# Projecting the recurrent branch's gates by seven block products inside the stream of projections

## The chip, the cores and the metric

The kernel runs on one core of a Trainium2 chip. The time is the device time of one execution in microseconds (us); lower is better. Beside it there is a profile of one execution, which lists every instruction of every engine with its start, its duration and what it waited for. The engines are TensorE (PE in the profile, its weight loads PEld), VectorE (DVE), ScalarE (ACT), GpSimd (POOL) and SyncE (SP). Each of them takes its instructions strictly in the order in which they stand in its own queue, and an instruction that waits holds up all behind it on that engine.

## The reference

One layer of a decoder trunk with 1024 rows (tokens) and 1024 channels. The normalised and modulated input `h` is projected by one large matrix; two branches of linear attention run on the result, each is gated by a SiLU gate, projected, merged by sigmoid gates and projected once more.

```python
proj = h @ w_in[l]
hq, hf, hi, hz, gq, gk, gv, gz, ga, mg = jnp.split(proj, IN_OFFSETS, axis=-1)

def hgrn2_branch(hq, hf, hi, hz, lb, norm_w):       # the recurrent branch, 8 heads of 128 channels
    q = jax.nn.silu(hq)
    f = lb + (1.0 - lb) * jax.nn.sigmoid(fr)        # fr is hf in float32
    k = (1.0 - lb) * jax.nn.sigmoid(-fr)
    o = chunked_gated_linear_attention(q, k, v, log_f, 1.0)
    o = rms_norm(o.reshape(B, T, HGRN_WIDTH), norm_w)
    return o * jax.nn.silu(hz)
```

What the change touches is `hz`, the projection behind the recurrent branch's gate: 1024 rows times 1024 columns with 1024 terms each, an eighth of it for each of the 8 heads, and the product `o * silu(hz)`.

## The kernel before, in words

**Products.** Every float32 factor of a product is split into a high part that the fast matmul format holds exactly and the low rest, by a copy on ACT and a subtraction on DVE (`split`, L196 and L197; the same pair of instructions stands at L1263/L1264 in `build` and at L1285/L1286 in `prep_duo`). A product is three matmuls: high times high, high times low, low times high.

**The stream.** After the normalisation of the rows a list of jobs runs (`Stream.go`). A `Feat` projects 128 columns for all 1024 rows: 8 steps over the terms, each of three products by two halves of the rows, 48 matmuls of 128x512 (L541), and then a closing function (`silu_done` at L952 and L953 for queries and gates, `hf_done` at L1077 to L1081 for the forget gates). The second branch's heads come first; then, for each recurrent head h from 0 to 7, the `Feat` of the query (hq), that of the forget gate (hf), for h = 0 and 4 the values of four heads (`Vblk2`), and the `Feat` of the gate (hz). `ahead` loads weights two jobs ahead and splits them one job ahead.

**The side tracks.** At each step of a job `weave` lets two queues of generators go on by a unit: the attention of the heads that have their inputs (scores at L683 to L781 on PE with masks and decays on DVE between them, L690 to L785; transposes L807; the products with the values L829, L848, L850), and in the back `gate_side` (the output gate, L1054) and `prepare`. `prepare` forms, for a later stage, sums of quarters of `h` (`factors`) and of quarters of the weights (`weight_sums`, four DVE additions L1195 to L1199 and four stores by POOL's queue, L1201, for each of 16 pieces), and waits while fewer than 12 buffers are free. A head's attention ends with `post`: on ACT a square (L1095), and on DVE `(attention * norm weight) * gate` (L1096).

**The last stages.** Four matrix products of 1024 x 1024 x 1024 (the two merging gates and the two branch projections) are each made by seven products of quarters instead of eight (`PRODUCTS`, in the order 1, 2, 5, 3, 6, 7, 4). A `Pair` holds the accumulator banks of two 128-column blocks; `Pair.run` is 12 matmuls of 128x512 for one product (L1343), and `Pair.after` carries sums from one product to the next: `snap_of` copies a bank to SBUF (L1315, L1317), `seed` copies such a copy back into a bank (L1323), `summed` adds on DVE (L1330). The output projection (L1520) closes the kernel.

**The order.** After the first 110 us or so no order written by hand holds: the tile framework's scheduler decides, when the kernel is built, where each instruction stands in its engine's queue. On the chip these queues are then fixed. In the rows of order shown below a name such as `b339_5089` is one buffer in one use, `pd124_4758` a pair of PSUM banks.

Of the kernel before, what the change touches and what calls it, by code (L numbers as in the profile page):

```python
# [31 lines left out]
OUT_PRODUCTS = (1, 5, 3, 6, 7, 2, 4)  # L32

# [50 lines left out]
def hybrid_trunk_kernel(  # L84
# [772 lines left out]
    class Stream:  # L857
# [186 lines left out]
    def gate_side():  # L1044

        gacc, gbias = S.get([D]), S.get([D])
# [38 lines left out]

    def hgrn_attention(h):
        st = h_state
        y = [None]
        sq = [None]

        def post(vh, half, po):
# [4 lines left out]
            nc.vector.scalar_tensor_tensor(y[0][:, sl], po, vec[:, R_HN + h:R_HN + h + 1],  # L1096
                                           y[0][:, sl], ALU.mult, ALU.mult)
# [5 lines left out]
        put_act(yh_d, h, y[0])  # L1103
        if ssq[0] is None:
            ssq[0] = sq[0]
        else:
            nc.gpsimd.tensor_add(ssq[0], ssq[0], sq[0])
            S.free(sq[0])
        if h == 7:
            yield 2  # L1110
            rst = S.get([T])
            yield from inverse_root(rst, ssq[0], D)
            S.free(ssq[0])
            rst_h[0] = rst

# [7 lines left out]
    for h in range(8):  # L1123
# [9 lines left out]
        J.append(Feat(col(C_HZ + h * P), rhs_h, silu_done(h_state, ("z", h))))  # L1133
# [19 lines left out]
    f_x = new_factors(h_d, "fx")  # L1153

    def factors(acts, f):
        sub = nc.vector.tensor_sub
        for kk in range(2):
            while len(S.free_list) < 12:
                yield 1
# [19 lines left out]
    sources += [[branch(n, d) for d in range(0, 8, 2)] for n in (1, 0)]  # L1179

    w_sums = [[[dp.tile([P, T], F32, name=f"ws{b}{j}{i}") for i in range(4)] for j in range(2)] for b in range(4)]

    def weight_sums(b, i):
        src = sources[b][i]
        while len(S.free_list) < 12:
            yield 1
# [12 lines left out]
        add(parts[3], parts[6], x2[:, :, 0])  # L1199
# [3 lines left out]
        S.free(x1, x2, s1, s2)  # L1203
        yield 3

    def prepare():
        yield from factors(h_d, f_x)
        for b in range(4):
# [15 lines left out]
    outs = [None] * 4  # L1224
# [45 lines left out]
    def load_duo(b, p, j):  # L1270

        t = raw_w[b, p, j] = S.get([2, 512])
        if p in SUMS:
            nc.sync.dma_start(t.rearrange("p a f -> p (a f)"), w_sums[b][j][SUMS[p]])
# [7 lines left out]
    def prep_duo(*duo):  # L1282
        t = raw_w.pop(duo)
        hi, lo = S.get([2, 512], F32R), S.get([2, 512], F32R)
# [3 lines left out]
        wt[duo] = (hi, lo)  # L1288

# [17 lines left out]
    class Pair:  # L1307
# [24 lines left out]

        def run(self, p):
            if p in (1, 5):
# [3 lines left out]
            h = H[0 if self.b == 1 else self.b, p]  # L1338
            for kt in range(4):
                h_hi, h_lo = (z[kt // 2][:, kt % 2, :] for z in h)  # L1340
                sl = slice(kt * P, (kt + 1) * P)
                for n, (a, c) in enumerate(((hi, h_hi), (hi, h_lo), (lo, h_hi))):
                    nc.tensor.matmul(o, a[:, sl], c, start=(p in (1, 5) and kt == 0 and n == 0),  # L1343
                                     stop=(kt == 3 and n == 2), skip_group_check=True)
                if kt % 2:
                    stream.weave(1)
# [3 lines left out]
        def after(self, p):  # L1350
            bank, snap, out = self.bank, self.snap, outs[self.b]
            if p == 1:
                if self.b:
# [88 lines left out]
    outs[:] = [put_gate1, put_gate0, put_t1, put_m]  # L1442
# [276 lines left out]
```

## Time and profile before

| | |
|---|---|
| median of 3 runs | 1215.8 us (1215.12 to 1216.45) |
| profiled execution: its time, its span | 1216.46 us, 1214.8 us |
| PE busy, share of the span | 1184.1 us, 97% |
| DVE | 790.9 us, 65% |
| ACT | 546.9 us, 45% |
| POOL | 123.8 us, 10% |
| stretch of the stream with the recurrent heads | 366 to 806 us |
| last stages, output stage | 806 to 1130 us, 1130 to 1207 us |

"Busy" counts an engine's instructions while they run. Consecutive instructions overlap a little at their ends, so that what a row of them costs in line is read from the distance of their starts. The time of a run is some 1.7 us longer than the span of its profile.

### The profile page before, as it was taken

The numbers are of one execution on the slowest core, as the hardware profiler recorded it, in microseconds if no ns is written. First come the engines' busy times: TensorE is split into PE (matmuls) and PEld (weight loads), VectorE is DVE, ScalarE is ACT, GpSimd is POOL, SyncE is SP. The second block draws the span as 40 slices with busy tenths as digits, with TensorE's granted clock in tenths as the row PEclk, the third lists the DMA queues.
The fourth block names the chain that finished last, engine by engine and source line by source line (L and its number), as shares of the span: only waits on it lengthen the run. The fifth ranks groups of instructions, "written<-read, shape, count | busy, mean of one in ns | idle before, by whom it ended". The sixth has DMA issues, their size and how long they took to land.

```text
span 1214.8 us, 20860 instructions
## 1 busy us (share of the span) xinstructions
PE 1184.1 (97%) x8579; PEld 982.6 (81%) x8579; DVE 790.9 (65%) x1245; ACT 546.9 (45%) x797; POOL 123.8 (10%) x215
## 2 busy tenths in 40 slices
PE   5999999999999999999999999999999999999997
PEld 3777889889798888888887888877778888878886
DVE  4637444774848456877884365794653775988994
ACT  5646732434434244344332324455743544444554
POOL 4100000202111121121110101011220000000000
PEclk9999999999999999999999999999999999999999
DMA  9814000844444267255341112054697746435523
GB/s 320 277 70 139 18 19 19 293 141 161 156 152 149 66 207 249 94 179 169 108 174 47 59 53 70 36 174 158 227 343 277 260 160 208 135 104 173 174 104 122
DMA packets 130961, 183.51 MB, mean 151 GB/s; under 512 B 7467, under 2 KB 97633, under 8 KB 130866
## 3 DMA queue, kind: packets, MB, share of 16 engines
q1 hardware_dynamic: 117250, 136.87, 35.7%
q0 software_dynamic: 13568, 45.31, 9.6%
q8 instruction: 67, 1.10, 0.4%
q14 instruction: 28, 0.23, 0.1%
q10 hardware_dynamic: 48, 0.01, 0.0%
HBM read 132.87 MB, written 49.28 MB: 150 GB/s over the span
## 4 chain that ended last, share of the span: by engine, by line
PE 61%; issue 23%; DVE 3%; ACT 3%; POOL 2%; DMA 1%; POOLq 0%; ACTq 0%; DVEq 0%
PE pd L541 19%; PE pd L1343 9%; PE sc_ps L1343 5%; PE pm L1343 5%; PE pd L1520 3%; PE pd L643 2%; PE pd L644 2%; PE pd L645 2%; PE sc_ps L1520 2%; PE pm L848 1%; PE pd L352 1%; PE pm L829 1%; PE pm L850 1%; PE pm L1520 1%; PE sc_ps L352 1%
## 5 line engine op out<-in xcount | busy, mean ns | idle before, releaser
L541 PE MATMUL pd<-b,b 128*128 128x512 f32 x1632 | 387.4, 394 | 0.0
L541 PEld LDWEIGHTS pd<-b,b 128*128 128x128 f32 x1632 | 302.4, 188 | 64.8 <-issue 1.4
L1343 PE MATMUL pd<-b,b 128*128 128x512 f32 x720 | 173.7, 392 | 4.3 <-ACT b L1414 2.1
L1343 PEld LDWEIGHTS pd<-b,b 128*128 128x128 f32 x720 | 133.7, 188 | 35.7 <-ACT b L1414 3.2
L197 DVE TENSOR_TENSOR b<-b,b 128x1024 fp32r<-128x1024 f32 (+2 forms) x89 | 98.9, 1122 | 83.1 <-ACT b L196 65.4
L196 ACT CAST b<-b 128x1024 fp32r<-128x1024 f32 (+2 forms) x89 | 82.9, 948 | 92.1 <-DVE b L1199 14.6
L1286 DVE TENSOR_TENSOR b<-b,b 128x1024 fp32r<-128x1024 f32 x56 | 68.3, 1224 | 66.9 <-ACT b L1285 52.3
L1285 ACT CAST b<-b 128x1024 fp32r<-128x1024 f32 x56 | 58.3, 1050 | 73.9 <-PE pd L1343 20.6
L1343 PE MATMUL sc_ps<-b,b 128*128 128x512 f32 x324 | 79.4, 391 | 1.0 <-ACT scT L793 1.0
L600 PE MATMUL pd<-b,b 128*128 128x256 f32 x256 | 74.2, 290 | 0.0
L1264 DVE TENSOR_TENSOR b<-b,b 128x1024 fp32r<-128x1024 f32 x48 | 59.2, 1251 | 20.8 <-ACT b L1263 15.1
L602 PE MATMUL pd<-b,b 128*128 128x256 f32 x256 | 72.5, 283 | 0.0
L601 PE MATMUL pd<-b,b 128*128 128x256 f32 x256 | 72.4, 283 | 0.0
L1343 PEld LDWEIGHTS sc_ps<-b,b 128*128 128x128 f32 x324 | 60.3, 188 | 14.6 <-ACT scT L793 1.4
L1343 PE MATMUL pm<-b,b 128*128 128x512 f32 x300 | 72.1, 389 | 0.0
L1263 ACT CAST b<-b 128x1024 fp32r<-128x1024 f32 x48 | 49.9, 1050 | 41.2 <-PE pd L1343 16.0
L1343 PEld LDWEIGHTS pm<-b,b 128*128 128x128 f32 x300 | 56.3, 188 | 11.7
L352 PE MATMUL pd<-b,b 128*128 128x512 f32 x192 | 53.3, 410 | 2.0 <-ACT b L196 0.9
L1201 POOL DMA_DIRECT2D ws<-b x64 | 34.6, 541 | 192.0 <-DVE b L1195 86.5
L735 ACT COPY xb<-b 128x512 f32<-128x512 f32 x48 | 29.4, 620 | 49.4 <-PE sc_ps L715 26.7
L643 PE MATMUL pd<-b,b 128*128 128x512 f32 x128 | 51.3, 401 | 0.0
L644 PE MATMUL pd<-b,b 128*128 128x512 f32 x128 | 50.0, 390 | 0.0
(285 smaller groups left out, 1964.3 us busy)
## 6 DMA issues: line engine op xcount, KB each, us to landing
b<-in_w_in_dram SPq DMA_DIRECT2D x66, 512.0 KB, 4.2
ws<-b POOLq DMA_DIRECT2D x64, 256.0 KB, 3.3
b<-ws SPq DMA_DIRECT2D x32, 512.0 KB, 4.9
b<-in_x_dram SPq DMA_DIRECT2D x16, 512.0 KB, 5.7
b<-in_ada_w_dram SPq DMA_DIRECT2D x32, 256.0 KB, 6.9
b<-in_w_branch_dram SPq DMA_DIRECT2D x16, 512.0 KB, 4.4
b<-h SPq DMA_DIRECT2D x14, 512.0 KB, 4.3
wo<-b POOLq DMA_DIRECT2D x14, 512.0 KB, 5.7
```

What stands on the lines that cost most here:

```text
L196: nc.scalar.copy(hi, src)
L197: nc.vector.tensor_sub(lo, src, hi.bitcast(F32))
L352: nc.tensor.matmul(accs[f], wg(a, d, f), b[d][:, half * 512:half * 512 + 512], start=(d == 0 and n == 0), stop=(d == KT - 1 and n == 2))
L541: nc.tensor.matmul(ps[0:w, th * 512:(th + 1) * 512], a[:, k, 0:w], b[:, th * 512:(th + 1) * 512], start=(k == 0 and n == 0), stop=(k == KT ...
L600: nc.tensor.matmul(o, lh, hi[:, k % 4, :], start=(k == 0), stop=False)
L601: nc.tensor.matmul(o, lh, lo[:, k % 4, :], start=False, stop=False)
L602: nc.tensor.matmul(o, ll, hi[:, k % 4, :], start=False, stop=(k == KT - 1))
L643: nc.tensor.matmul(o, lh, hi[:, k % 2, :], start=(k == 0), stop=False)
L644: nc.tensor.matmul(o, lh, lo[:, k % 2, :], start=False, stop=False)
L1286: nc.vector.tensor_sub(lo, t, hi.bitcast(F32))
L1343: nc.tensor.matmul(o, a[:, sl], c, start=(p in (1, 5) and kt == 0 and n == 0), stop=(kt == 3 and n == 2), skip_group_check=True)
L1520: nc.tensor.matmul(o, a, b, start=(p in (1, 5) and kt == 0 and n == 0), stop=(kt == 3 and n == 2), skip_group_check=True)
```

## The change

The eight gate `Feat`s of the recurrent heads (8 x 48 = 384 matmuls) go. In their place two jobs `Gates` stand in the stream, one behind hf of head 2 and one behind hf of head 6. Each makes the gates of four heads by the seven block products of the last stages: two `Pair`s, 7 products, 12 matmuls each, so 2 x 7 x 12 = 168, and 336 in both (L1462 in the changed file).

For that a `Gates` takes both pairs of PSUM accumulators that the `Feat`s use in turn, loads and splits seven weight pieces (three of them plain quarters, four of them sums that four further calls of `weight_sums` have to form earlier), fetches four pairs of summed factors and splits them (L197/L198, 8 splits; the plain quarters use the split input that is there), and runs `Pair.after`'s copies, seeds and sums (L1427, L1425, L1433, L1440). Its results leave by `put_z`: a sigmoid on ACT and a product on DVE for each 512 rows (L1145, L1146). While a `Gates` runs, `prepare` and `gate_side` pause, since they ask for more free buffers than there are; outside of it they ask for 10.

Heads 0, 1, 2 and 4, 5, 6 end their attention before or while their gate is made. Where it isn't there yet, ACT scales the attention's result (L1110), it is kept, and when gate and result both are there one product on DVE joins them (`gate_y`, L1092). Behind hf of head 7 there is no gate `Feat` any more, so this head's attention runs wholly inside the last stages.

Lines of the changed file are up to 120 further down than those of before; up to the scoring lines it is one line (L197 becomes L198, L541 becomes L542), L1343 becomes L1462, L1330 becomes L1440, L1317 becomes L1427.

**PE at the place of the first `Gates`.** Before, behind hf of head 2, the gate `Feat` of that head (accumulator `pd132`) begins:

```order
L541 MATMUL pd132_4977<-b5_143,b294_4897 128x512 x2
L541 MATMUL pd132_4977<-b13_151,b294_4897 128x512 x2
L541 MATMUL pd132_4977<-b5_143,b295_4898 128x512 x2
L541 MATMUL pd132_4977<-b6_144,b294_4897 128x512 x2
L541 MATMUL pd132_4977<-b14_152,b294_4897 128x512 x2
L541 MATMUL pd132_4977<-b6_144,b295_4898 128x512 x2
```

A product here needs the weights (`b294`, high part, `b295`, low part), split a job earlier. In the changed order the same queue stands as follows where product 6 of the first `Gates` gives way to product 7 (the accumulators are halves of `pd124` and `pd125`; `b322` to `b325`, `b334` and `b335` are split factors; `b328`, `b329` are product 6's weights and `b338` (high), `b339` (low) those of product 7):

```order
L1462 MATMUL pd124_4758<-b325_5012,b328_5032 128x512
L1462 MATMUL pd124_4758<-b324_5011,b329_5033 128x512
L1462 MATMUL pd124_4758<-b324_5011,b328_5032 128x512
L1462 MATMUL pd124_4758<-b325_5012,b328_5032 128x512
L1462 MATMUL pd124_4758<-b324_5011,b329_5033 128x512
L716 MATMUL sc_ps_72<-xb_142,b293_4750 32x48 x5
L1462 MATMUL pd125_4759<-b334_5080,b338_5088 128x512
L1462 MATMUL pd125_4759<-b335_5081,b338_5088 128x512
L1462 MATMUL pd124_4758<-b334_5080,b338_5088 128x512
L1462 MATMUL pd125_4759<-b334_5080,b339_5089 128x512
```

The third matmul of product 7 on `pd125` is the first that needs `b339`; ten matmuls of product 6 (the second pair's, with two short pieces of scoring) stand between the end of the first pair's product 6 and product 7.

**DVE at the same place.** Before, this part of DVE's queue, beside the same `Feat`, holds scoring, the gate's own product (L953) and weight sums:

```order
L699 TENSOR_TENSOR b301_4969<-b301_4969,b300_4968 128x256x3
L695 COPY_PREDICATED blk_141<-mask1_683,sc_ps_72 128x64
L696 COPY_PREDICATED blk_141<-mask1_683,sc_ps_72 128x64x2
L711 TENSOR_TENSOR xb_142<-xb_142,tot0_725 128x64x4
L697 COPY_PREDICATED blk_141<-mask1_683,sc_ps_72 128x64x2
L717 TENSOR_TENSOR b291_4849<-xb_142,tot0_725 128x64x12
L698 COPY_PREDICATED blk_141<-mask1_683,sc_ps_72 128x64
L953 TENSOR_TENSOR b309_5099<-b309_5099,pd132_4977 128x1024
L718 TENSOR_TENSOR tot0_725<-tot0_725 128x64
L1195 TENSOR_TENSOR b324_5384<-b317_5310 128x512
L719 TENSOR_TENSOR tot0_725<-tot0_725 128x64
L1198 TENSOR_TENSOR b323_5383<-b324_5384,b318_5311 128x512
```

In the changed order `b339` is written by the last of these rows. The first `Gates`' sum behind product 6 of the first pair (L1440 on `b333`) stands 13 rows ahead of it, followed by L691 and these:

```order
L700 TENSOR_TENSOR b293_4750<-b293_4750,b292_4749 128x256x3
L1146 TENSOR_TENSOR b307_4892<-b307_4892,b333_5072 128x512
L696 COPY_PREDICATED blk_141<-mask1_683,sc_ps_72 128x64
L1092 TENSOR_TENSOR b307_4892<-b307_4892,b279_4500 128x1024
L697 COPY_PREDICATED blk_141<-mask1_683,sc_ps_72 128x64x2
L198 TENSOR_TENSOR b347_5181<-b332_5057,b346_5180 128x1024
L198 TENSOR_TENSOR b337_5085<-b327_5016,b336_5084 128x1024
L698 COPY_PREDICATED blk_141<-mask1_683,sc_ps_72 128x64x2
L198 TENSOR_TENSOR b349_5185<-b330_5053,b348_5184 128x1024
L699 COPY_PREDICATED blk_141<-mask1_683,sc_ps_72 128x64
L1440 TENSOR_TENSOR b340_5151<-b340_5151,pd124_4758 128x512
L198 TENSOR_TENSOR b339_5089<-b321_5005,b338_5088 128x1024
```

Between the two stand the splits of product 4's weights and factors (`b347`, `b349`), of a factor of product 7 (`b337`), a gate's closing products (L1146, L1092), the second pair's sum (L1440) and scoring.

On ACT the copy that writes `b338` stands seven rows behind the copy of product 6's bank (L1427, to `b333`), and five of the rows between are copies for other splits.

**The second `Gates`, DVE.** The low part of product 7's weights is the last row here (`b490`); L1440 on the first pair's product 6 stands 19 rows ahead of it:

```order
L1092 TENSOR_TENSOR b460_6969<-b460_6969,b423_6480 128x1024
L198 TENSOR_TENSOR b488_7180<-b478_7070,b487_7179 128x1024
L757 COPY_PREDICATED blk_141<-mask4_700,sc_ps_72 128x8x4
L758 COPY_PREDICATED blk_141<-mask4_700,sc_ps_72 128x8x8
L744 TENSOR_TENSOR b444_6868<-b444_6868,tot0_725 128x32x16
L759 COPY_PREDICATED blk_141<-mask4_700,sc_ps_72 128x8x8
L745 TENSOR_TENSOR b437_6674<-b437_6674,tot0_725 128x32x16
L760 COPY_PREDICATED blk_141<-mask4_700,sc_ps_72 128x8x4
L757 COPY_PREDICATED blk_141<-mask4_700,sc_ps_72 128x8x4
L758 COPY_PREDICATED blk_141<-mask4_700,sc_ps_72 128x8x8
L744 TENSOR_TENSOR b444_6868<-b444_6868,tot0_725 128x16x32
L198 TENSOR_TENSOR b490_7184<-b472_7059,b489_7183 128x1024
```

Scoring of head 6 (L757 to L759, L744, L745) stands between them beside the splits. Two products earlier in the same job, the low part of product 5's weights (`b462`) is the last of these rows, behind the closing products of hf of head 6 (L1082 to L1084) and that head's scoring:

```order
L198 TENSOR_TENSOR b459_6954<-b448_6882,b458_6953 128x1024
L1082 TENSOR_SCALAR b443_6867<-b443_6867,oml_676,lb_675 128x1024
L1083 TENSOR_SCALAR b443_6867<-b443_6867 128x1024
L744 TENSOR_TENSOR b431_6550<-b431_6550,tot1_726 128x8x64
L745 TENSOR_TENSOR b420_6459<-b420_6459,tot1_726 128x8x64
L786 COPY_PREDICATED blk_141<-mask16_717,sc_ps_72 128x8x16
L1084 TENSOR_SCALAR b444_6868<-b444_6868,oml_676 128x1024
L677 TENSOR_TENSOR xb_142<-b437_6674,b443_6867 128x32x8
L678 TENSOR_TENSOR xb_142<-b437_6674,b443_6867 128x32x8x2
L198 TENSOR_TENSOR b462_6973<-b449_6885,b461_6972 128x1024
```

and PE needs it at the last of these rows, after one product's 12 matmuls and a transposition:

```order
L1462 MATMUL pd163_6876<-b8_146,b441_6769 128x512
L1462 MATMUL pd163_6876<-b16_154,b441_6769 128x512
L1462 MATMUL pd163_6876<-b8_146,b442_6770 128x512
L808 MATMUL pm165_6912<-ident_73,b431_6550 128x128 x4
L808 MATMUL pm166_6918<-ident_73,b431_6550 128x128 x3
L1462 MATMUL pd164_6877<-b456_6949,b461_6972 128x512
L1462 MATMUL pd164_6877<-b457_6950,b461_6972 128x512
L1462 MATMUL pd164_6877<-b456_6949,b462_6973 128x512
```

The diff, cut to its core:

```diff
@@ Stream.go
-                    if u >= 3 and u % 2:
+                    if u >= getattr(job, "late", 3) and u % 2:
@@ gate_side
+        while len(S.free_list) < room[0]:
+            yield 1
@@ hgrn_attention
             if half == 0:
-                y[0], sq[0] = st.pop(("z", h)), S.get([T])
+                y[0], sq[0] = st.pop(("z", h), None), S.get([T])
+                if y[0] is None:
+                    y[0], plain[0] = S.get([T]), True
...
+            if plain[0]:
+                nc.scalar.activation(y[0][:, sl], po, AF.Copy, scale=vec[:, R_HN + h:R_HN + h + 1])
+            else:
+                nc.vector.scalar_tensor_tensor(y[0][:, sl], po, vec[:, R_HN + h:R_HN + h + 1],
+                                               y[0][:, sl], ALU.mult, ALU.mult)
...
+    class Gates:
+        raws, parts, late = 1, 2, 20
...
+        def run(self):
+            j = self.j
+            two = [Pair(ZB, 2 * j + i) for i in range(2)]
+            room[0] = N_SLOTS
+            ps = [dtile(), dtile()]
+            R.free_list.extend(t[:, i * 512:i * 512 + 512] for t in ps for i in range(2))
+            load_duo(ZB, PRODUCTS[1], j)
+            self.fetch(5)
+            for n, p in enumerate(PRODUCTS):
+                if n + 2 < len(PRODUCTS):
+                    load_duo(ZB, PRODUCTS[n + 2], j)
+                if p in (2, 3):
+                    self.build({2: 5, 3: 6}[p])
+                if p in (5, 3, 6):
+                    self.fetch({5: 6, 3: 7, 6: 4}[p])
+                for i, pair in enumerate(two):
+                    yield from pair.steps(p)
+                    pair.after(p)
+                    if p == 5:
+                        pair.seed()
+                    if i == 0:
+                        if p in (6, 7):
+                            self.build({6: 7, 7: 4}[p])
+                        if n + 1 < len(PRODUCTS):
+                            prep_duo(ZB, PRODUCTS[n + 1], j)
...
@@ the list of jobs
-        J.append(Feat(col(C_HZ + h * P), rhs_h, silu_done(h_state, ("z", h))))
+        if h in (2, 6):
+            J.append(Gates(h // 4))
...
@@ prepare
-        for b in range(4):
+        for b in (ZB, 0, 1, 2, 3):
             for i in range(4):
                 yield from weight_sums(b, i)
```

More of the change, by code (lines that the diff above doesn't have):

```diff
@@ L1102, in hgrn_attention @@
             S.free(*st.pop(("v", h // 4)))
-        put_act(yh_d, h, y[0])
+        if plain[0]:
+            st[("y", h)] = y[0]
+            gate_y(h)
+        else:
+            put_act(yh_d, h, y[0])
         if ssq[0] is None:
@@ L1153, in hybrid_trunk_kernel @@
     f_x = new_factors(h_d, "fx")
+    room = [10]
     def factors(acts, f):
@@ L1157, in factors @@
         for kk in range(2):
-            while len(S.free_list) < 12:
+            while len(S.free_list) < room[0]:
                 yield 1
@@ L1331, in summed, with part, steps @@
             outs[self.b](2 * self.i + f, half, t, True)
+        def part(self, p, kt):
+            if self.b == ZB and p in (1, 2, 3):
+                kh, half = ((0, 0), (1, 0), (1, 1))[p - 1]
+                return [z[kh * 4 + kt][:, half * 512:half * 512 + 512] for z in (h_hi, h_lo)]
+            return [z[kt // 2][:, kt % 2, :] for z in H[0 if self.b == 1 else self.b, p]]
         def run(self, p):
+            for _ in self.steps(p):
+                stream.weave(1)
+        def steps(self, p):
             if p in (1, 5):
```

77 lines of the change are left out of this document (65 added, 12 removed).

## The prediction

> **What bounds the kernel now.** I read the page first (busy shares, then the costliest groups), then the stretches of the program one by one, the waits of PE in the stream, and the timelines of PE and DVE at the place of the change.
>
> ```profile
> PE 1184.1 (97%) x8579; PEld 982.6 (81%) x8579; DVE 790.9 (65%) x1245; ACT 546.9 (45%) x797; POOL 123.8 (10%) x215
> L541 PE MATMUL pd<-b,b 128*128 128x512 f32 x1632 | 387.4, 394 | 0.0
> L1343 PE MATMUL pd<-b,b 128*128 128x512 f32 x720 | 173.7, 392 | 4.3 <-ACT b L1414 2.1
> ```
>
> PE is busy 97% of the span, and the stream's matmuls (L541) had no idle time before them. By stretches (columns: stretch, its length, busy PE, PEld, DVE, ACT, POOL, granted clock, DMA share, GB/s):
>
> ```profile
> 450.00:614.00 164.00, 163.41 (x1629) 135.90 (x1628) 123.97 (x236) 64.88 (x109) 26.32 (x42) 1.00 0.47 152
> 535.00:550.80 15.80, 15.80 (x129) 12.79 (x127) 15.68 (x27) 3.24 (x5) 3.19 (x6) 1.00 0.76 252
> 870.00:1130.00 260.00, 257.74 (x1132) 211.34 (x1131) 185.68 (x197) 121.86 (x153) 13.41 (x25) 1.00 0.63 208
> ```
>
> So matmuls that go are time that goes, as long as nothing makes PE wait in their place. DVE has room on average (124 of 164 us in the first heads), but none just where the first `Gates` comes: 535 to 550.8 is the gate `Feat` of head 2, and there DVE worked 15.7 of 15.8 us. PE didn't wait for it, because what a `Feat` needs was split a job earlier. The waits of PE between 366 and 806 us are these two:
>
> ```profile
> PE pm L829 <- ACT b L808: 0.4, 1, 0.4
> PE sc_ps L715 <- DVE blk L698: 0.2, 1, 0.2
> ```
>
> **What the change takes away.** 384 matmuls against 336. The price of one, from the timeline of PE at that `Feat` (start, duration, line, count):
>
> ```profile
> 531.60 11.18 PE L541 MATMUL pd<-b,b 128*128 128x512 f32 x48
> 542.71 1.31 PE L683 MATMUL sc_ps<-xb,b 128*32 128x80 f32 x64
> 543.95 7.09 PE L541 MATMUL pd<-b,b 128*128 128x512 f32 x30
> 551.24 0.89 PE L715 MATMUL sc_ps<-xb,b 128*32 128x48 f32 x64 [0.20 <-DVE blk L698]
> 552.06 8.45 PE L541 MATMUL pd<-b,b 128*128 128x512 f32 x36
> ```
>
> From start to start 48 take 11.11 us, 0.23 each. The 48 that go are worth 11.1 us, all of it on the path. Scoring costs 1.24/64 = 0.02 (L683) and 0.82/64 = 0.013 (L715) per matmul.
>
> **What it adds: product 7 has to wait.** The `Feat`s had a job's time for splitting. A `Gates` has one product's, two pairs by 12 matmuls, 24 x 0.23 = 5.5 us, for one weight split, two factor splits and the sums, with the attention's scoring in the same queue. The order shows where this ends last: at product 7. PE's third matmul of it needs `b339`, the low part of its weights, and DVE makes this 13 rows behind the sum (L1440) that itself waits for the first pair's product 6. The prices are from DVE's timeline at the start of the last stages, where the same lines run back to back, by start to start:
>
> ```profile
> 806.08 1.23 DVE L1286 TENSOR_TENSOR b<-b,b 128x1024 fp32r<-128x1024 f32 x1
> 807.21 1.23 DVE L1264 TENSOR_TENSOR b<-b,b 128x1024 fp32r<-128x1024 f32 x1
> ...
> 811.75 0.43 DVE L690 TENSOR_TENSOR blk<-sc_ps,eye 128x256 f32<-128x256 f32 x1
> 812.08 0.96 DVE L699 TENSOR_TENSOR b<-b,b 128x768 f32<-128x768 f32 x1
> 812.95 0.45 DVE L695 COPY_PREDICATED blk<-mask,sc_ps 128x64 f32<-128x64 int32 x1
> 813.13 0.56 DVE L696 COPY_PREDICATED blk<-mask,sc_ps 128x128 f32<-128x128 int32 x1
> 813.47 0.74 DVE L710 TENSOR_TENSOR xb<-b,tot 128x512 f32<-128x512 f32 x1
> 814.11 0.46 DVE L697 COPY_PREDICATED blk<-mask,sc_ps 128x128 f32<-128x128 int32 x1
> 814.34 0.47 DVE L711 TENSOR_TENSOR xb<-xb,tot 128x256 f32<-128x256 f32 x1
> 814.71 0.45 DVE L698 COPY_PREDICATED blk<-mask,sc_ps 128x64 f32<-128x64 int32 x1
> 814.88 1.34 DVE L1286 TENSOR_TENSOR b<-b,b 128x1024 fp32r<-128x1024 f32 x1
> ...
> 817.61 0.28 DVE L721 TENSOR_TENSOR tot<-tot 128x64 f32<-128x64 f32 x1
> 817.93 0.60 DVE L746 TENSOR_TENSOR tot<-tot 128x32 f32<-128x32 f32 x3
> 818.52 0.96 DVE L720 TENSOR_TENSOR b<-b,tot 128x768 f32<-128x768 f32 x1
> 819.39 0.19 DVE L756 COPY_PREDICATED blk<-mask,sc_ps 128x32 f32<-128x32 int32 x1
> 819.49 0.23 DVE L757 COPY_PREDICATED blk<-mask,sc_ps 128x64 f32<-128x64 int32 x1
> 819.62 0.69 DVE L744 TENSOR_TENSOR b<-b,tot 128x512 f32<-128x512 f32 x1
> 820.23 0.22 DVE L758 COPY_PREDICATED blk<-mask,sc_ps 128x64 f32<-128x64 int32 x1
> ```
>
> A 1024 wide row costs 1.13, a 512 wide one 0.60 (819.62 to 820.23), and the copy of a bank on ACT, as the last stages make it (L1317), this:
>
> ```profile
> L1317 ACT ACTIVATE b<-pd 128x512 f32<-128x512 f32 x12 | 7.0, 592 | 4.7 <-PE pd L1343 4.7
> L1263 ACT CAST b<-b 128x1024 fp32r<-128x1024 f32 x39 | 40.6, 1049 | 34.4 <-PE pd L1343 16.0 <-DMA b<-fx 5.1 <-PE pm L1343 5.0
> ```
>
> First `Gates`, counted from the end of the first pair's product 6: the copy 0.59; then on DVE L1440 0.60, L691 0.33, L700 0.87, L1146 0.60, L696 0.18, L1092 1.13, L697 0.34, two splits 2.26, L698 0.23, a split 1.13, L699 0.17, L1440 0.60, and the split of `b339` 1.23 to its end: 10.3 us. ACT isn't later: its copy of the high part comes behind four wide copies and two narrow ones, about 5 x 1.05 + 3 x 0.59 = 7.0. PE has meanwhile ten matmuls of product 6, three of product 7 (13 x 0.23 = 3.0) and twelve short ones (0.2). It waits 10.3 - 3.2 = **7.1 us**, in two pieces (for the high part, then for the low one).
>
> Second `Gates`, the same join, DVE's 19 rows behind L1440 there: copy 0.59, L1440 0.60, the three short kinds L722 and L747 0.9, five 1024 or 768 wide rows and the 512 wide L1146 among them (1.13 + 0.60 + 0.87 + 1.13 + 1.13 = 4.9), scoring L757 to L745 with three wide ones (0.1 to 0.13 each, 0.61 each wide) 2.5, the split of `b490` 1.23: 10.7 us. PE has 14 matmuls and 32 short ones, 3.2 + 0.4 = 3.6. It waits **7.1 us**. Both ends for either wait: zero (DVE takes these rows while PE is still at product 6, which the order excludes, since the sum at their head waits for product 6 itself) and 10.7. I take the sums, as they are rows of exactly these kinds.
>
> **At product 5 of the second `Gates`** PE needs `b462` after 14 matmuls and a transposition like this one:
>
> ```profile
> 831.68 0.92 PE L807 MATMUL pm<-ident,b 128*128 128x128 f32 x7
> ```
>
> That is 14 x 0.23 + 0.9 = 4.1 us behind the scoring matmuls (L782) with which the `Gates` begins. DVE's rows from the first that needs these, L744, to `b462` are two of 512 at 0.60, L786 0.2, L1084, L677 and L678 (bounded by 0.60 and 1.13 each, mostly the first) and the split 1.23: 4.4 to 6.0. L1082 and L1083 ahead of them, up to 1.13 each, may be done by then or not. So the wait is between 0.3 and 4.2 us; I take **2.0**.
>
> **What else it adds.** Per `Gates` 15 splits instead of 4, eight sums and eight gate products of 512, against four gate products of 1024 (L953) saved: on DVE 11 x 1.13 + 16 x 0.60 - 4 x 1.13 = 17.5 us more within PE's 45 us. What is put off meets the next head's transpositions and values behind the `Gates` (L808, L830, L849 of the changed file). PE waited 0.6 us in all for such things in this stretch before; the other bound is the 17.5. I take 1.5 each, **3.0**, near the low end, as DVE was idle 40 us of 164 there. The weight sums are the same DVE and POOL work moved from one place of the queue to another, with 4 more of them: 4 x 4 x 0.60 = 9.6 us of DVE and 16 stores on POOL's queue, under PE's matmuls of the heads; if that cover goes they appear in the 1.5. They are queued on POOL and the fetches on SP; the weight piece of product 7 is asked for two products early (11 us), against 4.9 us that such a load takes:
>
> ```profile
> b<-ws SPq DMA_DIRECT2D x32, 512.0 KB, 4.9
> ```
>
> **Behind the stream.** Head 7's attention has eight steps of a `Feat` less to hide under and runs with the first groups of the last stages, whose DVE is 71% busy (185.7 of 260). Before, PE lost 64.0 - 61.0 = 3.0 us between 806 and 870:
>
> ```profile
> 806.00:870.00 64.00, 60.99 (x508) 48.64 (x508) 40.40 (x62) 39.64 (x60) 6.29 (x8) 1.00 0.50 177
> 811.90 5.73 PE L1343 MATMUL pd<-b,b 128*128 128x512 f32 x24 [1.49 <-DVE b L953]
> ```
>
> The 1.49 for L953, head 7's gate, goes; more scoring joins comes. I take **+0.5**, with ends -1.5 and +3. ACT's plain scaling in place of a DVE product, and `gate_side`'s eight DVE rows at a later place, lie off PE's path; I cost them at nothing.
>
> **Sum.** -11.1 + 7.1 + 7.1 + 2.0 + 3.0 + 0.5 = +8.6 us. The profiled execution took 1216.46 us, 0.7 over the median; against the median, 1215.8 + 8.6 = 1224.4. I say 1224.5.
>
> **The rivals.** *Faster.* DVE and ACT keep up at the two product 7s, PE runs through, and of the 11.1 us only 3 to 4 of the smaller waits are lost: 1208 to 1209. For it: the same block products run in the last stages (the row 870 to 1130) with PE waiting 2.3 us in 260 while DVE is busy 71%. Against it: there no scoring stands in DVE's queue and four pairs, not two, share each factor's split. It decides at a sum of waits of 11 us: `b339` and `b490` would have to come 2.5 us sooner each, and product 5 without a wait.
>
> *The clock gate.* PE's first matmuls after the sparse start ran at half rate, later ones at full; behind the last matmul the granted clock fell:
>
> ```profile
> 19.17 2.07 PE L352 MATMUL pd<-b,b 128*128 128x512 f32 x4 [0.20 <-ACT b L196]
> 30.41 1.07 PE L352 MATMUL pd<-b,b 128*128 128x512 f32 x4
> 1210.00:1215.00 5.00, 0.00 (x0) 0.00 (x0) 0.45 (x1) 0.42 (x1) 0.00 (x0) 0.50 0.28 107
> ```
>
> After the 1.49 us wait quoted above 24 matmuls took 5.73, so so short a pause does not do it. If waits of 4 to 7 us do, matmuls behind each run at half rate for some us. The slow start shown lasted at least the 2.07 us of one such row, which costs half of it, 1.0 us; as two pieces each time, at two places, it is 4 more, and with a slow stretch of 5 us up to 10: 1228 to 1234. The Trainium skill ("TensorE: Matmul & The Clock Gate", the section "HAM oscillation — how this bites in real kernels") warns against PE gaps over about 3.4 us, and its Part 1 gives about 3.4 us of slow matmuls after one; by it each 7 us wait would cost an estimated 1.7 more, 3.4 in all, 1228. No trace here yet shows a long wait in mid kernel.
>
> *The tail.* Head 7's attention, no longer begun under a `Feat`, holds up the banks that the first groups of the last stages lend from it (`side_done`): up to 6 instead of 0.5, 1230.
>
> *No difference.* The change does what it says on PE but its waits happen to make up the 11.1: 1213.4 to 1218.2. 0.2% of 1215.8 is 2.4 us, about what a measurement of this kernel can tell from no change.
>
> **How the numbers follow.** Forecast (slower by 4 to 13) 0.57; clock gate 0.17; tail 0.07; no difference 0.07; faster 0.12. Slower by over 0.2%: 0.57 + 0.17 + 0.07 = 0.81; same 0.07; faster 0.12. The two long waits (5 each if two of the wide rows between are done earlier, 10.7 at their end), the 0.3 to 4.2 at product 5, 0.5 to 3 each behind the `Gates` and the gate's 4 to 10 take the range to 1213 below, the border of the no-difference case, and 1235 above; by sign alone slower is 1219 to 1235.
>
> **What would show it.** In the profile after: L1462 with 336 more matmuls on the halves of `pd` where L541 has 384 fewer; idle time before L1462 of 7 us at each product 7, ended by L198 on DVE (and by L197 on ACT for the first piece); about 2 us at product 5 of the second; PE's busy time some 11 us less in the stream and the span longer nonetheless. Wrong would be: idle time below 5 us in all before L1462 in the two `Gates` (then faster), a granted clock of 1.00 with matmuls of 0.23 right behind the waits (no clock gate), or waits that sum to 14 us but are made up elsewhere.

## The result, and the profile after

The changed kernel takes 1248.3 us (median of 5 runs, 1243.7 to 1249.7) against 1216.5 (5 runs, 1215.1 to 1217.6): slower by the factor 1.0258, 95% interval 1.0244 to 1.0272. The forecast was 1224.5, with 1235 as its upper end: the direction was right, the size was not. The profiled execution has a span of 1246.6 us against 1214.8, 31.8 us more, and a mean granted clock of 0.985 against 0.998.

The page of the changed kernel, PE's row and its two largest groups:

```profile
PE 1188.9 (95%) x8531; PEld 981.8 (79%) x8531; DVE 825.9 (66%) x1295; ACT 582.5 (47%) x851; POOL 131.7 (11%) x231
L542 PE MATMUL pd<-b,b 128*128 128x512 f32 x1248 | 300.9, 397 | 0.0
L1462 PE MATMUL pd<-b,b 128*128 128x512 f32 x1056 | 263.6, 401 | 14.2 <-ACT b L197 4.4
```

PE has 48 matmuls fewer and is busy 4.8 us longer (1188.9 to 1184.1), where 11.1 less were due. The rest of its span grew from 30.7 to 57.7 us, 27.0 more. The two together are the 31.8.

Where it lies is seen from the starts of the stages, the first matmul of each, taken from the two traces (the values' projection of heads 0 to 3 is L643 before and L644 after):

| from | to | before | after | difference |
|---|---|---|---|---|
| first `Feat` (L541) | values of heads 0 to 3 | 279.5 us | 291.9 | +12.4 |
| values of heads 0 to 3 | last stages | 415.9 | 435.3 | +19.3 |
| last stages | output stage | 324.3 | 325.4 | +1.1 |

Of the loss, 12.4 us come before any `Gates` has begun. Stretches of the changed kernel (the first is the second branch's heads, the second and third hold one `Gates` each; the eighth column is the granted clock):

```profile
110.00:366.00 256.00, 247.50 (x2146) 219.18 (x2145) 149.50 (x250) 104.56 (x140) 26.30 (x42) 0.97 0.37 122
515.00:577.50 62.50, 54.68 (x536) 42.73 (x534) 47.63 (x84) 35.31 (x55) 4.57 (x5) 0.92 0.32 105
741.00:804.00 63.00, 54.71 (x578) 43.64 (x577) 47.24 (x79) 32.12 (x51) 4.57 (x5) 0.95 0.40 127
```

The trace also dates the drops of the granted clock. It is 0.50 from 246.9 to 253.7, 322.0 to 328.8, 557.5 to 567.8, 786.2 to 793.0 and 844.2 to 847.7 us, and 1.00 between them; in the kernel before it is 1.00 from 22 us to behind the last matmul. PE is busy in 24.6 us of these five stretches, so they account for at most half of that, 12.3 us, of longer work.

PE's waits over the whole run, the largest that are new:

```profile
PE sc_ps L716 <- DVE tot L719: 8.5, 2, 5.6
PE sc_ps L716 <- DVE blk L699: 6.1, 1, 6.1
PE pd L1462 <- ACT b L197: 4.4, 2, 4.0
PE pd L1462 <- DVE b L198: 4.0, 2, 2.5
PE pm L830 <- ACT b L809: 3.3, 4, 1.3
PE pd L1462 <- ACT b L1081: 3.0, 1, 3.0
```

The second to the fourth belong to the joins of product 6 and product 7; 1.5 of the fourth's 4.0 us are the wait at product 5 of the second `Gates`. PE's timeline at the first join, then at product 5 and the join of the second `Gates`:

```profile
553.22 1.67 PE L1462 MATMUL pd<-b,b 128*128 128x512 f32 x6
560.96 0.53 PE L716 MATMUL sc_ps<-xb,b 128*32 128x48 f32 x10 [6.07 <-DVE blk L699]
561.87 8.50 PE L1462 MATMUL pd<-b,b 128*128 128x512 f32 x24 [0.39 <-ACT b L197]
...
749.62 0.73 PE L1462 MATMUL pd<-b,b 128*128 128x512 f32 x2 [1.50 <-DVE b L198]
...
781.51 0.89 PE L716 MATMUL sc_ps<-xb,b 128*32 128x48 f32 x64
786.41 1.22 PE L1462 MATMUL pd<-b,b 128*128 128x512 f32 x2 [4.01 <-ACT b L197]
790.12 8.20 PE L1462 MATMUL pd<-b,b 128*128 128x512 f32 x29 [2.49 <-DVE b L198]
```

PE waits 6.5 us at each join. Behind the first wait 24 matmuls take 8.50 us, 0.35 each instead of 0.23; behind the second, 29 take 8.20, 0.28 each.

The first row of the list, 8.5 us, was in no part of the forecast. It lies in the second branch's heads. DVE's timeline there, and PE's:

```profile
235.10 1.22 DVE L198 TENSOR_TENSOR b<-b,b 128x1024 fp32r<-128x1024 f32 x1
244.07 0.69 DVE L1289 TENSOR_TENSOR b<-b,b 128x512 f32<-128x512 f32 x1 [7.76 <-DMA b<-in_w_in_dram]
244.68 0.68 DVE L711 TENSOR_TENSOR xb<-b,tot 128x512 f32<-128x512 f32 x1
```

```profile
236.43 7.09 PE L542 MATMUL pd<-b,b 128*128 128x512 f32 x30
249.08 1.51 PE L716 MATMUL sc_ps<-xb,b 128*32 128x48 f32 x64 [5.55 <-DVE tot L719]
250.51 9.97 PE L542 MATMUL pd<-b,b 128*128 128x512 f32 x36
```

L1289 is an addition of `weight_sums`. It stands ahead of a head's scoring in DVE's queue and waits 7.8 us for its piece of the weights; the scoring behind it is free to go and can't. The load itself was late because, by the profile, the store of a summed factor still held its buffer. SP's queue waited to issue it, between 200 and 260 us:

```profile
SPq L1282 <- DMA fx<-b: 11.2, 2, 10.3
```

A second wait of 2.9 us at L716 follows 74 us later, where L1288 waits 3.2 us for a store of the second branch's result.

### The profile page after: what moved, and what is told of

Its sections match the earlier page's. It is cut to its first block, busy times and chain, and to the rows that moved or that the text cites. A ratio compares the mean times of both kernels' runs of the same rounds, so it can differ in the third digit from the quotient of the medians.

```text
span 1246.6 us, 21016 instructions
## 1 busy us (share of the span) xinstructions
PE 1188.9 (95%) x8531; PEld 981.8 (79%) x8531; DVE 825.9 (66%) x1295; ACT 582.5 (47%) x851; POOL 131.7 (11%) x231
## 3 DMA queue, kind: packets, MB, share of 16 engines
q0 software_dynamic: 14848, 49.50, 10.2%
## 4 chain that ended last, share of the span: by engine, by line
PE 69%; issue 10%; DVE 5%; DMA 4%; ACT 4%; POOL 2%; SPq 0%; POOLq 0%; ACTq 0%; DVEq 0%
PE pd L542 16%; PE pd L1462 16%; PE sc_ps L1462 5%; PE pm L1462 5%; PE pd L1639 3%; PE pd L644 2%; PE pd L646 2%; PE pd L645 2%; PE pm L849 2%; PE pd L603 2%; PE pd L602 2%; PE pd L601 2%; PE pm L830 2%; PE sc_ps L1639 2%; PE pm L851 2%
## 5 line engine op out<-in xcount | busy, mean ns | idle before, releaser
L542 PE MATMUL pd<-b,b 128*128 128x512 f32 x1248 | 300.9, 397 | 0.0
L1462 PE MATMUL pd<-b,b 128*128 128x512 f32 x1056 | 263.6, 401 | 14.2 <-ACT b L197 4.4
L542 PEld LDWEIGHTS pd<-b,b 128*128 128x128 f32 x1248 | 233.8, 190 | 51.6 <-issue 2.2
L1462 PEld LDWEIGHTS pd<-b,b 128*128 128x128 f32 x1056 | 199.3, 192 | 61.6 <-DVE b L198 6.0
L198 DVE TENSOR_TENSOR b<-b,b 128x1024 fp32r<-128x1024 f32 (+2 forms) x111 | 125.4, 1144 | 95.4 <-ACT b L197 70.5
L197 ACT CAST b<-b 128x1024 fp32r<-128x1024 f32 (+2 forms) x111 | 105.6, 967 | 115.7 <-DMA b<-in_w_in_dram 14.0
L1389 DVE TENSOR_TENSOR b<-b,b 128x1024 fp32r<-128x1024 f32 x56 | 68.1, 1221 | 57.7 <-ACT b L1388 44.6
L1462 PE MATMUL sc_ps<-b,b 128*128 128x512 f32 x324 | 78.5, 391 | 0.3 <-ACT scT L794 0.3
L1462 PE MATMUL pm<-b,b 128*128 128x512 f32 x300 | 72.1, 389 | 0.0
L1462 PEld LDWEIGHTS sc_ps<-b,b 128*128 128x128 f32 x324 | 60.4, 188 | 13.8 <-ACT scT L794 0.6
L1297 POOL DMA_DIRECT2D ws<-b x80 | 43.2, 541 | 264.9 <-DVE b L1288 88.7
L1462 PEld LDWEIGHTS pm<-b,b 128*128 128x128 f32 x300 | 56.3, 188 | 11.7
L353 PE MATMUL pd<-b,b 128*128 128x512 f32 x192 | 53.2, 409 | 1.8 <-ACT b L197 0.9
L644 PE MATMUL pd<-b,b 128*128 128x512 f32 x128 | 51.4, 401 | 0.0
L646 PE MATMUL pd<-b,b 128*128 128x512 f32 x128 | 49.9, 390 | 0.0
L645 PE MATMUL pd<-b,b 128*128 128x512 f32 x128 | 49.9, 390 | 0.0
```

The source lines that it names most:

```text
L197: nc.scalar.copy(hi, src)
L198: nc.vector.tensor_sub(lo, src, hi.bitcast(F32))
L542: nc.tensor.matmul(ps[0:w, th * 512:(th + 1) * 512], a[:, k, 0:w], b[:, th * 512:(th + 1) * 512], start=(k == 0 and n == 0), stop=(k == KT ...
L644: nc.tensor.matmul(o, lh, hi[:, k % 2, :], start=(k == 0), stop=False)
L645: nc.tensor.matmul(o, lh, lo[:, k % 2, :], start=False, stop=False)
L646: nc.tensor.matmul(o, ll, hi[:, k % 2, :], start=False, stop=(k == KT - 1))
```

## The experiments

**Which part makes the loss ahead of the `Gates`.** The change lowers the number of free buffers that `factors` and `weight_sums` ask for from 12 to 10. First run: the changed kernel with that start put off again.

```diff
@@ factors
-            while len(S.free_list) < room[0]:
+            while len(S.free_list) < max(12, room[0]):
@@ weight_sums
-        while len(S.free_list) < room[0]:
+        while len(S.free_list) < max(11, room[0]):
```

> The changed kernel, but `factors` starts only with 12 free buffers, as before, and `weight_sums` with 11 instead of 10. Theory A (about 12 us of the loss arise far ahead of the Gates, in the second branch's heads, where a weight sum that waits for its load stands ahead of scoring in DVE's queue, because these sums now start a few buffers earlier): PE's two waits at L716 (5.6 and 2.9 us) go, the recurrent heads' values start some 12 us earlier, and the time is about 1236 (1233 to 1240). Rival (the four extra sums or the Gates' fetches themselves cost those 12 us): the waits stay in another place, 1245 to 1250.

1239.4 us (1238.8 to 1243.6); to before 1.0200 (1.0177 to 1.0223). The stretch ahead of the values is 279.1 us, as before; between 112 and 395 us PE's only wait is

```profile
PE sc_ps L716 <- DVE tot L719: 0.3, 1, 0.3
```

The 12.4 us are gone, as theory A has it. But the time falls by 9, not by 12: in the profiled execution, the slowest of these runs, the heads' stretch is 2.2 us longer than in the changed kernel and the last stages 6.5, with other waits (2.9 at L1462 on ACT in the second `Gates`, 2.4 at L830).

Second run: the kernel before, with nothing changed but the room.

```diff
-            while len(S.free_list) < 12:
+            while len(S.free_list) < 10:
```

The same in `weight_sums`.

> The kernel before with nothing changed but that `factors` and `weight_sums` ask for 10 free buffers instead of 12. There are no Gates and no extra sums. Theory A: the same two waits at the scoring (L715) appear, about 8 us of idle PE and 3 to 4 us of slow matmuls behind them: 1226 to 1229. Rival (the room alone is harmless): 1214 to 1218.

1235.6 us (1234.2 to 1239.4), 1.0167 (1.0144 to 1.0189): more than theory A said. The wait ahead of the scoring is back, in this trace of DVE

```profile
243.41 0.69 DVE L1196 TENSOR_TENSOR b<-b,b 128x512 f32<-128x512 f32 x1 [6.74 <-DMA b<-in_w_in_dram]
```

and PE's list has 10.1 us for this line, 7.5 of them ahead of the values, with a wait of 3.9 at a later head:

```profile
PE sc_ps L715 <- DVE tot L718: 10.1, 3, 5.4
PE sc_ps L770 <- DVE blk L759: 3.9, 1, 3.9
```

Of the 19.5 us, 8.5 are lost ahead of the values and 9.8 in the heads' stretch. So the number alone, without a single `Gates`, costs over half of what the whole change does.

Two more runs bound this. The kernel before with the four extra weight sums, unused, and the room at 12:

```diff
-        for b in range(4):
+        for b in (4, 0, 1, 2, 3):
```

> The kernel before, with the four extra weight sums (those of the gates' weights) formed ahead of the others and used by nothing; the room stays 12. Theory A (the start of the sums, not their number, costs the time ahead of the Gates): 1215 to 1219. Rival (the extra sums push the later ones into a place where their loads hold up scoring): 1221 to 1230, with waits of PE between 450 and 806 us.

1219.7 us (10 runs, 1216.2 to 1223.1), 1.0030 (1.0018 to 1.0041): 3.8 us more, between the ranges of theory A and of the rival. In the profiled execution, the fastest of the ten, the stretch ahead of the values is 279.4 us, as before. The extra sums alone cost little. And the kernel before with 14 in place of 12, in `factors` and in `weight_sums`:

```diff
-            while len(S.free_list) < 12:
+            while len(S.free_list) < 14:
```

> The kernel before with 14 free buffers asked for instead of 12, the step to the other side of the run with 10. Theory A (the sums cost time where they start so early that their buffers are still being stored): starting later, they hold up nothing in the second branch's heads; 1213 to 1220. Rival (the order that the scheduler makes at 12 is a good one by chance, and any other room costs): 1224 to 1240.

1226.2 us (1225.1 to 1227.8), 1.0081 (1.0064 to 1.0098). The time lies in the rival's range. Theory A is right about the second branch's heads, which run without the long waits (280.6 us), and still the heads' stretch is 10.6 us longer. Its longest wait is for ACT's transposition copies, which cost PE 0.4 us in the kernel before; here they stand behind scoring copies and a split that end late:

```profile
575.08 3.35 PE L829 MATMUL pm<-b,b 128*128 128x128 f32 x14 [3.36 <-ACT b L808]
```

So theory A holds for what stands ahead of the `Gates`, but "start later and nothing is held up" does not: each number gives another order and other waits, and 12 is the best of the three. That 12 is good by chance, as the rival has it, three numbers don't show.

**The clock behind the waits.** 28 matmuls whose result nothing uses, into a free bank between product 6 and product 7 of each `Gates`:

```diff
+                    if p == 6 and i == 1:
+                        idle = R.get()
+                        for _ in range(28):
+                            nc.tensor.matmul(idle, h_hi[0][:, 0:P], h_hi[0][:, 0:512], start=True, stop=True,
+                                             skip_group_check=True)
+                        R.free(idle)
```

> The changed kernel with 28 matmuls of 128x512 into an unused bank (their results are used by nothing) between product 6 and product 7 of each Gates, 6.4 us of work just where PE waits 6.5. Theory B (a wait of that length lets TensorE's clock fall, and the matmuls behind it then run at half rate): the 24 matmuls behind the first wait take 5.6 us instead of 8.5, those behind the second 6.8 instead of 8.3 or so, and although 56 matmuls are added the time falls by 3 to 6 us, to 1242 to 1245. Rival (the matmuls behind the waits are slow because they still wait for their weights): same, or up to 3 us slower, 1247 to 1251, and those rows stay at 8.5.

1245.2 us (1241.2 to 1249.3), 1.0241 (1.0211 to 1.0270); the two kernels' ranges overlap, so the time alone decides little. The traces do. PE at the two joins (L1196 is the added work, L1468 the blocks' line):

```profile
554.24 6.53 PE L1196 MATMUL pd<-b 128*128 128x512 f32 x28
560.71 0.38 PE L716 MATMUL sc_ps<-xb,b 128*32 128x48 f32 x16
561.25 1.20 PE L1468 MATMUL pd<-b,b 128*128 128x512 f32 x4 [0.17 <-ACT b L197]
562.38 0.53 PE L716 MATMUL sc_ps<-xb,b 128*32 128x48 f32 x26
562.84 4.87 PE L1468 MATMUL pd<-b,b 128*128 128x512 f32 x20
...
780.24 6.64 PE L1196 MATMUL pd<-b 128*128 128x512 f32 x28
786.71 0.61 PE L1468 MATMUL pd<-b,b 128*128 128x512 f32 x2
788.04 6.89 PE L1468 MATMUL pd<-b,b 128*128 128x512 f32 x29 [0.71 <-DVE b L198]
```

The 24 matmuls take 6.1 us, not 8.5, and the 29 take 6.9, not 8.2, though the same splits are due on DVE and ACT. The granted clock is 1.00 from 540 to 600 and from 770 to 860 us, where the changed kernel has its last three stretches at 0.50. PE's busy time is 1196.3 us: 7.4 more than in the changed kernel for 56 matmuls, which are 12.9 us, so 5.5 us of slow work went in the whole run. Theory B is shown. On top of the later sums the same 28 matmuls:

> The run with later sums and the 28 unused matmuls between product 6 and product 7 of each Gates. Theory B (the clock falls in these waits): the same gain as they brought to the changed kernel, 3 to 4 us, on top of the later sums: 1234 to 1238, with matmuls of 0.23 behind both joins. Rival (no clock effect): 1239 to 1243.

1236.3 us (1233.5 to 1241.6), 1.0172 (1.0143 to 1.0201), 3 us under the later sums alone, as theory B had it; again the ranges overlap. Behind both joins the matmuls take some 0.24 us each, and the granted clock stays at 1.00.

**Product 7's wait.** Its weights split ahead of the first pair's matmuls instead of behind them:

```diff
+                if n + 1 < len(PRODUCTS):
+                    prep_duo(ZB, PRODUCTS[n + 1], j)
                 for i, pair in enumerate(two):
...
-                        if n + 1 < len(PRODUCTS):
-                            prep_duo(ZB, PRODUCTS[n + 1], j)
```

> The changed kernel, but in a Gates the weights of the next product are split ahead of the first pair's matmuls of the present one, not behind them: twelve matmuls (2.8 us) earlier. Theory C (product 7 waits only for the rows that stand between product 6's sum and its splits on DVE): product 7's weights now come ahead of that sum, its second factor is the last to come, two to four rows earlier, and each of the two waits shrinks from 6.5 to 4 to 5.5 us; 1243 to 1247. Rival (DVE as a whole is full inside a Gates): the waits turn up at other products, 1247 to 1250.

1257.0 us (1254.3 to 1259.5), 1.0333 (1.0305 to 1.0360): slower still. The waits at product 7 did shrink, to 2.1 and 2.3 us, but the rival is right in a stronger form: what was put behind is late elsewhere, most of all ACT's copies behind the transposes (L809), which PE's L830 needs:

```profile
PE pm L830 <- ACT b L809: 11.8, 4, 7.1
PE pd L1462 <- DVE b L1440: 3.7, 1, 3.7
```

A `Gates` without the DVE products that end a gate takes work out instead of moving it:

```diff
         nc.scalar.activation(z_sl, ap, AF.Sigmoid)
-        nc.vector.tensor_mul(z_sl, z_sl, ap)
...
-            nc.vector.tensor_mul(z, z, y)
```

> The changed kernel without the DVE products that end a gate: `put_z` leaves the sigmoid as it is (no L1146) and `gate_y` doesn't multiply (no L1092); the output is another. Theory C (product 7 waits for the rows between product 6's sum and its splits on DVE): by the rows that are left there, 0.59 on ACT, then on DVE 0.60, 0.64, 0.33, 0.87, three splits at 1.13 to 1.23 and four short ones, 1.1 in all, 7.6 us against 3.2 us of matmuls: the first wait falls from 6.5 to about 4.4 us, and the time by 4 to 7 us, to 1241 to 1245. Rival (the wait hangs on the load of product 7's weights or on ACT): it stays at 6 to 6.5 and the time at 1246 to 1249.

1238.7 us (1236.7 to 1239.1), 1.0182 (1.0162 to 1.0201), 10 us less than the changed kernel, more than expected. At the first join

```profile
556.24 0.74 PE L1460 MATMUL pd<-b,b 128*128 128x512 f32 x2 [3.22 <-ACT b L197]
557.69 6.90 PE L1460 MATMUL pd<-b,b 128*128 128x512 f32 x22 [0.71 <-DVE b L198]
```

PE waits 3.9 us against 4.4 by the rows, and 3.6 at the second join: the rows of DVE and ACT between product 6's sum and product 7's splits set this wait. The stretches at half clock behind the joins are 3.4 us each, against 10.2 and 6.8, and PE's list has no wait for hf of head 7 (L1081, 3.0 us in the changed kernel). Both help to explain the surplus.

**Work moved to POOL.** On top of the later sums, the weight pieces' low parts and L1092 by POOL:

```diff
-            wt[duo] = split_raw(t)
+            hi, lo = S.get([2, 512], F32R), S.get([2, 512], F32R)
+            nc.scalar.copy(hi, t)
+            nc.gpsimd.tensor_sub(lo, t, hi.bitcast(F32))
...
-            nc.vector.tensor_mul(z, z, y)
+            nc.gpsimd.tensor_mul(z, z, y)
```

> As the run with later sums, but inside a Gates the low parts of the seven weight pieces, and the closing product of gate and result (L1092), are made by POOL instead of DVE: 7 to 10 rows of 1024 fewer in DVE's queue per Gates. Theory C (product 7 waits for the rows that stand between product 6's sum and its splits on DVE): some four 1.13 us rows less stand in that stretch, each of the two waits falls from 6.5 to 2 to 4 us, and the clock no longer falls behind them: 1225 to 1232. Rival (POOL, which takes 2.4 us for such a row, is late instead of DVE): product 7 waits as long or longer, 1237 to 1245.

1257.8 us (1256.0 to 1260.2), 1.0339 (1.0321 to 1.0357), 18 us more than with DVE and above the rival's range too. At the joins PE waits 11.6 and 11.3 us instead of 6.5, as the rival had it. POOL and DVE at the first join:

```profile
542.67 2.35 POOL L1092 TENSOR_TENSOR b<-b,b 128x1024 f32<-128x1024 f32 x1 [6.21 <-DVE b L1146]
544.99 3.06 POOL L1387 TENSOR_TENSOR b<-b,b 128x1024 fp32r<-128x1024 f32 x1
```

```profile
543.03 2.81 DVE L700 TENSOR_TENSOR b<-b,b 128x768 f32<-128x768 f32 x1
545.76 0.43 DVE L698 COPY_PREDICATED blk<-mask,sc_ps 128x128 f32<-128x128 int32 x1
546.00 2.33 DVE L712 TENSOR_TENSOR xb<-xb,tot 128x256 f32<-128x256 f32 x1
```

While POOL works, two of DVE's rows take 2.81 and 2.33 us that took 0.96 and 0.47 (L699 and L711 before), and each ends 0.3 to 0.8 us after a POOL row ends. With 14 unused matmuls at the joins as well:

> As the run with the splits on POOL, with 14 unused matmuls (3.2 us, their results used by nothing) between product 6 and product 7 of each Gates. If waits are left there that are shorter than these or a little longer, the matmuls fill them and keep the clock up: the same as that run or up to 4 us less. If the waits are gone, the 28 matmuls lie on the path: up to 6 us more.

1257.1 us (1253.6 to 1260.6), 1.0332 (1.0305 to 1.0359): no difference that can be told from the run without them. The waits there, 11.6 and 11.3 us, were far longer than 3.2.

**One `Gates` at a time**, the other four heads with `Feat`s, both on top of the later sums. The second alone, as shown, and the first alone with `h // 4 != 0` and `h == 2`:

```diff
-        if h in (2, 6):
-            J.append(Gates(h // 4))
+        if h // 4 != 1:
+            J.append(Feat(col(C_HZ + h * P), rhs_h, silu_done(h_state, ('z', h))))
+        if h == 6:
+            J.append(Gates(h // 4))
```

> As the run with later sums (room 12 and 11), but heads 0 to 3 get their gates by four Feats as before; only the second Gates (heads 4 to 7) is left, with its half of the saved matmuls. Theory (each Gates loses more by its own waits and the slow matmuls behind them than its 24 matmuls, 5.5 us, save): the later-sums run is 23 us over before, a half of that stays here: 1225 to 1230. Rival (the loss lies in what both share, the extra sums and the stream's order around them): 1234 to 1240, near the run with both.

> The mirror of the run with the second Gates alone: heads 4 to 7 get their gates by four Feats, the first Gates is left. Theory (each Gates carries its own loss): 1224 to 1230, and the two single runs' distances from before add up to that of the run with both, 23 us, within 4. Rival (shared cause): 1234 to 1240; or, if the loss hangs on head 7, whose gate Feat is back here, close to before, 1214 to 1219.

The second alone: 1235.9 us (1235.6 to 1236.4), 1.0158 (1.0143 to 1.0173). The first alone: 1232.5 (1230.0 to 1234.0), 1.0134 (1.0117 to 1.0152). Their distances from before, 18.9 and 15.5, add up to 34, not to the 23 of both. That each `Gates` carries its own loss is not true. The second alone lies in the range of the rival, a shared cause; the first alone lies in no range. In the second's trace one of the two largest waits is at the join of its `Gates` (5.4 us), the other comes before it, behind the values of heads 4 to 7. ACT, then PE:

```profile
676.90 1.04 ACT L197 CAST b<-b 128x1024 fp32r<-128x1024 f32 x1 [9.07 <-DMA ws<-b]
```

```profile
681.86 3.36 PE L830 MATMUL pm<-b,b 128*128 128x128 f32 x14 [5.17 <-ACT b L809]
```

A split for the next job waits 9.1 us on ACT for the store of a weight sum, with an attention's copies (up to L809) queued behind it. It is the same pattern as L1289 on DVE. What the shared loss consists of beyond such waits was not taken apart further.

## Why the prediction was wrong in size

By its own terms:

- **The 48 matmuls, -11.1 us.** They went. PE's busy time shows nothing of it, because its other work grew longer (the last point).
- **Product 7, 7.1 + 7.1.** 6.5 and 6.5. The order shown in the change's section and the prices of the rows gave the length; the row that ended the first wait was the scoring that stood two rows ahead of the split (L699, then L716 on PE), not the split itself. The run without the gates' products bears the mechanism out.
- **Product 5 of the second `Gates`, 2.0.** 1.5.
- **What else, 3.0.** The other waits between the values and the last stages come to 6.3 us, of which 0.7 stood there before. Idle time there grew by 20.0 us in all, against the 19.2 that the terms for product 7, product 5 and this one make together.
- **Behind the stream, +0.5.** The stage table has +1.1. The wait for L953 went as forecast, one of 3.0 us for hf of head 7 (L1081) came in its place.
- **The weight sums: the step that failed.** The prediction called them "the same DVE and POOL work moved from one place of the queue to another" under PE's matmuls, and left their cover to the 1.5 us behind a `Gates`. It counted their work and not what they wait for, nor did it follow the lowered room to the second branch's heads, some 270 us ahead of the first `Gates`. There they cost 12.4 us: idle time grew by 7.8, and 4.6 are slower matmuls behind the waits, where the granted clock is 0.50. The later sums took these 12.4 us away, and the lowered room alone brought 8.5 back to the same stretch in the kernel before.
- **The clock: a rival, with a chance of 0.17, that came true.** In the heads' stretch the matmuls saved and the idle time make -11.1 + 20.0 = 8.9; the stretch grew by 19.3, so 10.4 us are longer PE work. The granted clock is 0.50 there at the two joins alone, with 10.6 us of busy PE in it, which makes at most 5.3 us of the 10.4; that size is within the 4 to 10 of the rival. Of the other 5 us the clock is not the cause. Matmuls that run less often in unbroken rows are a guess; no run separated it.

The sum that came out, from the forecast's 8.6: 12.4 ahead of the `Gates`, 10.4 of longer PE work, 0.8 of idle time in the heads' stretch, 0.6 behind it in the last stages, and -1.0 at the two ends of the program add 23.2 and give 31.8. The prediction's rules for the clock stood apart from its likeliest case, though the waits on which that case rested were long enough to bring the clock down: the two belonged together. With the clock's 5 us in it the number would have been about 1230 (1215.8 + 8.6 + 5.3), well inside the range, and the sums' 12.4 would have taken it out, to about 1242. The waits at product 7 were near their terms because the rows were read rightly. That all idle time agrees to 1 us, 20.0 against 19.2, is partly luck: the waits at products 7 and 5 came out 1.7 us under their terms and the small ones 2.6 over theirs.

## What to carry to other kernels

- A change that moves preparing work earlier moves its waits too. For each moved instruction on an in-order engine, ask what it waits for (a load, and behind the load the store that still holds its buffer) and what stands behind it; its busy time may be the smallest part of its price.
- Follow thresholds on free buffers through the whole program, not only through the stage that the change is for. Here 10, 12 and 14 gave 1235.6, 1216 and 1226 us in an otherwise untouched kernel.
- Where a forecast has TensorE waiting for several us in mid kernel, price the slower matmuls behind it in the same case.

## What was not expected of the hardware

TensorE's clock falls behind shorter waits than the forecast thought. The later sums' second `Gates` has

```profile
740.44 5.49 PE L1462 MATMUL pd<-b,b 128*128 128x512 f32 x12 [2.89 <-ACT b L1427]
```

0.46 us a matmul, twice the usual 0.23, behind a wait of 2.9 us; in the run with the filled waits 24 matmuls behind a wait of 2.9 us took 5.82, the full rate. The Trainium skill ("TensorE: Matmul & The Clock Gate", Part 1) says that the windows in which activity is counted run freely, of about 3.4 us each. The traces agree: in all fourteen, every stretch at 0.50 in mid kernel lasts one to four times 3.41 us, and the time between two such stretches is a whole multiple of 3.41 us too. That fits a wait of 2.9 us that sometimes counts and sometimes doesn't, and a spread of 6 us between runs of the changed kernel where the kernel before has 2.5. Of PE's waits in these traces those of 3.4 us and more all led into such a stretch or lay in one, those between 2.0 and 3.4 us did so in most cases, and the kernel before, with none above 1.9 in mid kernel, has no such stretch.

Beside POOL rows of 1024 elements two of DVE's rows ended only after them (2.81 and 2.33 us instead of 0.96 and 0.47), while other rows, such as L698 at 0.43, ran at their usual length. It goes by the kind of row: in that run 14 of the 28 TENSOR_TENSOR rows of DVE that overlap a POOL row with two inputs take 1.9 to 3.1 us, and none of the 19 SCALAR_TENSOR_TENSOR rows does.
